# Three mask copies on ScalarE instead of GpSimd, and a shorter memset, in one inference step of a hybrid decoder

## The chip, the cores and the metric

The kernel runs on one core of one Trainium2 chip. The metric is device time in microseconds (us), the median of several runs; less is better. Engines in the profile: PE is TensorE (matmuls and transposes), PEld its weight loads, DVE is VectorE, ACT is ScalarE, POOL is GpSimd, SP is SyncE, which issues most of the DMAs. Each engine works through its own instruction stream in order; engines wait for each other by semaphores.

## The reference, cut to what matters

One decoder layer for a prompt of 1024 tokens and 8 decode samples. A projection `w_in` (1024 x 3480) feeds three groups of heads: an NSA group (compressed blocks, selected blocks, sliding window), an RWKV-7 group and a memory cross-attention; the groups are gated, concatenated and projected back.

```
q_raw, kv_raw, g_raw, z_nsa, u_rw, z_rw, q_mem, z_mem = split_in(rms_norm(x, ln_g) @ w_in)
ck, cv = compress(rows4[:, :2])          # blocks of 32 rows, stride 16, a small MLP
s_c = q @ ck * SCALE, masked by cend <= qpos      # uses cmask
s_s = q @ k_sel, s_w = q @ k_win (window 512)     # masked by bmask
o = g0 * softmax(s_c) @ cv + g1 * softmax(s_s) @ v_sel + g2 * softmax(s_w) @ v_win
y = x + concat(o * silu(z_nsa), o_rw * silu(z_rw), o_mem * silu(z_mem)) @ w_out
```

The change is in how the two masks of the prompt's attention are brought from DRAM into their final tiles. `bmask` (128 x 1152, bf16) is an additive mask: its first 128 columns hold the edge of the window, the last 128 the causal triangle, and the 896 between them are zero. `cmask` (128 x 248) holds the mask of the compressed scores as two matmul operands.

## The kernel before, in words

The kernel has three phases. Phase 1 projects the prompt in column blocks of `w_in` (the matmuls named `p_pr`, in split precision: `whi`, `wlo` by `hi`, `lo`), and weaves into these blocks, by written-out generators, the RWKV recurrence, the memory's keys and values, the turning of the attention's keys, and the compression of the prompt's K/V rows. Phase 2 is the prompt's attention, phase 3 the samples' and the output projection. TensorE's order is written out by hand: `InOrder` (line 77) chains every matmul and transpose behind the one before (line 86, `_do`), so that TensorE can take nothing out of turn.

The change is in `prompt_cmp` (line 1308), the generator of the compression, which runs near the end of phase 1. It does the following, in program order.

- Line 1311 takes the slot `c4` for the tile `c_am` (128 x 504, f32), and line 1312 loads the three masks' data into it with one DMA on SP's queue. `slot` (line 1271) gives out one buffer for each name `c0` to `c7`: a later tile of the same name must wait until all users of the earlier one are done.
- Lines 1313 to 1318 fill `bmask`, a one-column tile `one`, and `cmask`, all on GpSimd. The three copies (lines 1315, 1316, 1318) read `c_am`.
- Lines 1319 to 1327 load the compression's weights and the rows to compress (`px`).
- Lines 1332 to 1342 turn those rows: four groups of four transposes write `p_xt`, and ScalarE copies each group to a tile `pxt` (line 1340). The first of these, `pxt0`, takes the slot `c4` again, which `c_am` has held. So the first `pxt` copy can't start before the last reader of `c_am` is done.
- `p_xt` and the turned keys `p_k` share the PSUM pool `pw`, which has three buffers (line 499). The third `p_xt` takes the buffer that the first `pxt` copy frees.

Around it stand other generators: `turn_keys` (line 1282) turns keys (`p_k`), splits them on ScalarE (`kh`, line 1294) and VectorE (`kl`, line 1295); `cmp_consts` (line 1062) turns the position encoding (`p_pe`), copies it on VectorE (`peT`, line 1073) and multiplies it by the weights (`p_pc`); `do_z` (line 312) evicts the gate columns (`zt`, lines 317 and 318). GpSimd also issues the stores of the RWKV output (`y_d`, line 1040), ahead of the masks in its stream.

The masks' first use is in phase 2: `bmask` in line 1478 and `cmask` in line 1394.

Of the kernel before, what the change touches and what calls it, by code (L numbers as in the profile page):

```python
# [14 lines left out]
AF = mybir.ActivationFunctionType  # L15
# [98 lines left out]
class Step:  # L114
# [1193 lines left out]
    def prompt_cmp(self):  # L1308
        nc, I, O = self.nc, self.I, self.O
        V, A, G, PE = nc.vector, nc.scalar, nc.gpsimd, self.te  # L1310
        am = self.slot(4, [128, 504], F32, "c_am")
        nc.sync.dma_start(am[:], I["c_at"][:, 0:504])
        G.memset(self.bmask[:], 0.0)
        G.memset(self.one[:], 1.0)
        G.tensor_copy(self.bmask[:, 0:128], am[:, 128:256])
        G.tensor_copy(self.bmask[:, 1024:1152], am[:, 0:128])
        self.cmask = self.kt.tile([128, 248], F32R, name="cmask")
        G.tensor_copy(self.cmask[:], am[:, 256:504])
        self.load_w1([self.slot(e, [128, 8, 2, 64], F32, f"w1s{e}") for e in range(2)])
        xs = []  # L1320
        src = O["nsa_rows_prompt"]
        for e in range(2):
            x = self.slot(2 + e, [128, 2, 8, 64], F32, f"px{e}")
            for g in range(2):
                nc.sync.dma_start(x[:, g], bass.AP(tensor=src.tensor, offset=src.offset + (2 * e + g) * 64,
                                                  ap=[[8 * 512, 128], [512, 8], [1, 64]]))
            xs.append(x)
        yield 4.0
        consts = self.cmp_consts()
        self.spawned.append(consts)  # L1330
        xts = []
        for e in range(2):
            xt = self.slot(4 + e, [128, 4, 2, 128], F32, f"pxt{e}")
            for jj in range(0, 4, 2):
                ps = self.pw.tile([128, 2, 2, 128], F32, name="p_xt", tag="w")
                for j in range(2):
                    for g in range(2):
                        PE.transpose(ps[:, j, g, :], xs[e][:, g, 2 * (jj + j):2 * (jj + j) + 2, :].rearrange("p a b -> p (a b)"),
                                     self.ident[:])
                A.activation(xt[:, jj:jj + 2], ps[:], AF.Copy)  # L1340
                yield
            xts.append(xt)
        hid = self.wk.tile([128, 2, 64], F32, name="phid")
        while consts.gi_frame:
            yield 0.5
        yield from self.compress(lambda e, m: xts[e][:, m % 4, :, m // 4::2], 2, hid)
        self.spawned.append(self.mem_turn())
        ck, cv = self.cmp_out(hid[:].rearrange("p n c -> p (n c)"))
        yield 6.0
        self.k_stack(ck, 1, self.ck[:, :, 0, :], self.ck[:, :, 1, :])  # L1350

        nc.gpsimd.memset(self.cvk[:], 0.0)
        for g in range(2):
            r = slice(g * 64, g * 64 + 64)
            A.activation(self.cvk[r, g], cv[r], AF.Copy)
        yield 4.0
# [1228 lines left out]
```

## Time and profile before

| | |
|---|---|
| runs | 929.98, 935.8, 934.21 us; median 934.21 |
| the profiled execution | 932.48 us, its span 930.7 us, mean granted TensorE clock 0.994 |
| busy PE / PEld | 890.9 us (96%) / 756.6 us (81%) |
| busy DVE / ACT / POOL | 645.9 us (69%) / 439.6 us (47%) / 189.9 us (20%) |
| DMA | 107.01 MB, mean 115 GB/s |

The rows of the profile's views are read like this. A row of a timeline has start and busy time in us, the engine, the line of the kernel, the operation, output and inputs, shapes, and the number of instructions merged; in brackets stands the engine's idle time before it and what ended it. Line 86 is the helper through which all of TensorE's work goes, so tiles tell more there than lines. A row of waits has the waiting engine and tile, what it waited for, then the total in us, the number of times and the longest. Matmuls are pipelined, so a row's busy time is longer than the distance to the next row's start; distances between starts are the better measure.

### The profile page before, as it was taken

To read this page: it belongs to the slowest core of one execution; us is meant where nothing else is said; L and a number is where in the kernel's file an instruction comes from. 1 tells how busy PE (TensorE), PEld (TensorE's weight loads), DVE (VectorE), ACT (ScalarE), POOL (GpSimd) and SP (SyncE) were. 2 spreads that over 40 slices of the span, in tenths; PEclk is the share of its full clock that TensorE was granted. 3 is DMA by queue.
4 is the path that set the end of the run, shared out by engine and by line. 5 is a ranking of instruction groups with operands and counts; after the bars stand their busy time and mean duration, and the time that the engine had idled before them with its cause. 6 is when DMAs were issued, how large, how long until landed. Compare 5 with 4: busy or idle time off the path is not lost.

```text
span 930.7 us, 24648 instructions
## 1 busy us (share of the span) xinstructions
PE 890.9 (96%) x9839; PEld 756.6 (81%) x9839; DVE 645.9 (69%) x2002; ACT 439.6 (47%) x1003; POOL 189.9 (20%) x283
## 2 busy tenths in 40 slices
PE   8999999999999999988998999999999998999998
PEld 8998888977878788757986788888887877887976
DVE  7768679954777459945556876666778986548454
ACT  7654324232443233223536577667567776324211
POOL 2000000000000000001103544454445766112010
PEclk9999999999999999999999999999999999999999
DMA  8521314141321204524738413332130027986561
GB/s 281 133 74 35 105 36 121 51 115 48 89 82 53 76 14 133 134 84 121 183 102 231 137 59 120 106 117 66 33 87 13 29 81 209 307 259 213 177 236 48
DMA packets 128298, 107.01 MB, mean 115 GB/s; under 512 B 26385, under 2 KB 113112, under 8 KB 128056
## 3 DMA queue, kind: packets, MB, share of 16 engines
q1 hardware_dynamic: 123096, 93.43, 34.3%
q0 software_dynamic: 3296, 10.75, 3.3%
q8 instruction: 78, 1.28, 0.6%
q10 hardware_dynamic: 1792, 1.26, 0.4%
q14 instruction: 36, 0.29, 0.1%
HBM read 84.72 MB, written 22.78 MB: 116 GB/s over the span
## 4 chain that ended last, share of the span: by engine, by line
PE 67%; DVE 18%; ACT 5%; issue 4%; DMA 3%; POOL 2%; SPq 1%; DVEq 0%; ACTq 0%; POOLq 0%
PE p_pr L86 24%; PE p_out L86 8%; PE p_s L86 5%; PE p_o L86 5%; PE p_pT L86 4%; PE p_pr L306 2%; PE p_hid L86 2%; ACT p L1485 2%; DVE p L1478 2%; DMA wraw<-in_w_in_dram 2%; PE p_it L86 1%; DVE wlo L283 1%; PE p_tk L86 1%; PE p_iy L86 1%; DVE pt L1446 1%
## 5 line engine op out<-in xcount | busy, mean ns | idle before, releaser
L86 PE MATMUL p_pr<-h,whi 128*128 128x512 f32 (+2 forms) x1168 | 282.2, 335 | 2.0 <-DVE zt L318 2.0
L86 PEld LDWEIGHTS p_pr<-h,whi 128*128 128x128 f32 x1168 | 190.2, 190 | 22.1 <-issue 2.8
L86 PE MATMUL p_pr<-h,wlo 128*128 128x512 f32 (+2 forms) x584 | 188.9, 326 | 1.1 <-DVE wlo L283 1.1
L1516 POOL TENSOR_SCALAR p<-p,fac,gates 128x640 f32<-128x640 f32 (+7 forms) x128 | 104.2, 826 | 89.4 <-DVE fac L1512 56.0
L86 PEld LDWEIGHTS p_pr<-h,wlo 128*128 128x128 f32 x584 | 109.8, 189 | 11.3 <-DVE wlo L283 1.5
L1485 ACT ACTIVATE p<-p,nm 128x640 f32<-128x640 f32 (+7 forms) x128 | 93.1, 729 | 40.7 <-DVE nm L1478 37.4
L86 PE MATMUL p_pT<-ident,p 128*128 128x128 f32 x528 | 71.9, 279 | 8.8 <-DVE pt L1446 4.0
L1104 POOL MEMSET w2d<- 128x128 f32 x1 | 0.2, 205 | 376.8 <-PE p_iy L86 376.8
L86 PEld LDWEIGHTS p_pT<-ident,p 128*128 128x128 f32 x528 | 56.6, 140 | 21.6 <-issue 5.9
L86 PE MATMUL p_o<-pt,vs 128*64 128x128 f32 x1056 | 67.9, 276 | 0.4 <-DVE cat L1554 0.4
L86 PE MATMUL p_s<-kh,qs 128*128 128x512 f32 (+3 forms) x191 | 64.8, 352 | 1.8 <-DVE nm L1478 1.6
L1478 DVE CUSTOM_DVE_ANT_0 p<-p_s,bmask 128x512 f32<-128x512 f32 (+7 forms) x96 | 60.6, 661 | 7.6 <-PE p_s L86 6.1
L282 ACT ACTIVATE whi<-wraw 128x1024 fp32r<-128x1024 f32 x34 | 36.0, 1059 | 62.3 <-PE p_pr L86 48.8
L86 PEld LDWEIGHTS p_o<-pt,vs 128*64 128x64 f32 x1056 | 57.0, 137 | 7.7 <-issue 4.2
L283 DVE TENSOR_TENSOR wlo<-wraw,whi 128x1024 fp32r<-128x1024 f32 x33 | 40.3, 1221 | 33.0 <-ACT whi L282 32.9
L86 PE MATMUL p_s<-kl,qs 128*128 128x512 f32 (+3 forms) x192 | 60.4, 334 | 0.0
L1446 DVE COPY pt<-p_pT 128x512 f32<-128x512 f32 (+1 forms) x72 | 48.2, 673 | 11.7 <-PE p_pT L86 11.5
L86 PE MATMUL p_out<-woh,chi 128*128 128x512 f32 x128 | 51.7, 404 | 0.0
L86 PE MATMUL p_out<-woh,clo 128*128 128x512 f32 x128 | 50.2, 392 | 0.4 <-DVE clo L2421 0.4
L86 PE MATMUL p_out<-wol,chi 128*128 128x512 f32 x128 | 49.9, 390 | 0.0
L1444 ACT ACTIVATE pt<-p_pT 128x512 f32<-128x512 f32 (+1 forms) x72 | 41.1, 577 | 14.2 <-PE p_pT L86 13.6
L86 PEld LDWEIGHTS p_s<-kh,qs 128*128 128x128 f32 x191 | 36.1, 189 | 5.5 <-DVE nm L1478 3.0
(546 smaller groups left out, 1779.5 us busy)
## 6 DMA issues: line engine op xcount, KB each, us to landing
wraw<-in_w_in_dram SPq DMA_DIRECT2D x34, 512.0 KB
pg<-in_c_pool_dram SPq DMA_DIRECT2D x32, 256.0 KB
pg<-in_c_pool_dram SPq DMA_DIRECT2D x48, 128.0 KB
x<-in_x_prompt_dram SPq DMA_DIRECT2D x8, 512.0 KB
z_d<-zt SPq DMA_DIRECT2D x16, 256.0 KB
cat<-z_d SPq DMA_DIRECT2D x8, 512.0 KB
xres<-in_x_prompt_dram POOLq DMA_DIRECT2D x16, 256.0 KB, 3.6
out_dram<-xres POOLq DMA_DIRECT2D x16, 256.0 KB, 3.0
```

What stands on the lines that cost most here:

```text
L86: self.last = getattr(self.engine, op)(*a, **k)
L282: nc.scalar.activation(hi[:, :, :n], raw[:, :, :n], AF.Copy)
L283: (low or nc.vector).tensor_tensor(lo[:, :, :n], raw[:, :, :n], hi[:, :, :n].bitcast(F32), op=OP.subtract)
L306: self.last_mm = self.pe.matmul(ps[:m, :b - a], w[:, k, :m], h[k][:, a:b], start=(k == 0 and i == 0), stop=(k == 7 and i == 2))
L1104: nc.gpsimd.memset(w2d[:], 0.0)
L1444: nc.scalar.activation(pt[:, :n], ps[:, :n], AF.Copy)
L1446: nc.vector.tensor_copy(pt[:, :n], ps[:, :n])
L1478: return V.tensor_tensor_reduce(halves(x), halves(ps), m, -1.0, 3.0e38, op0=OP.add, op1=OP.min, accum_out=nm[:, h, b:b + 1])
L1485: e = A.activation(x, x, AF.Exp, scale=-1.0, bias=nm[:, h, b:b + 1], accum_out=sm[:, h, b:b + 1])
L1516: nc.gpsimd.tensor_scalar(x, x, f[:, h, b:b + 1], gate[:, hd + h, 1 + b:2 + b], op0=OP.mult, op1=OP.mult)
```

## The change

ScalarE (`A`) makes the three copies out of `c_am`, as activations with the function Copy, instead of GpSimd (`G`); GpSimd's memset of `bmask` covers only the 896 middle columns, which the copies don't write.

```
-        G.memset(self.bmask[:], 0.0)
+        G.memset(self.bmask[:, 128:1024], 0.0)
         G.memset(self.one[:], 1.0)
-        G.tensor_copy(self.bmask[:, 0:128], am[:, 128:256])
-        G.tensor_copy(self.bmask[:, 1024:1152], am[:, 0:128])
+        A.activation(self.bmask[:, 0:128], am[:, 128:256], AF.Copy)
+        A.activation(self.bmask[:, 1024:1152], am[:, 0:128], AF.Copy)
         self.cmask = self.kt.tile([128, 248], F32R, name="cmask")
-        G.tensor_copy(self.cmask[:], am[:, 256:504])
+        A.activation(self.cmask[:], am[:, 256:504], AF.Copy)
```

On ScalarE, near the end of phase 1, between the eviction of a gate block (`zt`) and the first copy of the turned rows (`pxt`), the stream changes so:

```order
 L317 ACTIVATE zt<-p_pr 128x256
 L317 ACTIVATE zt<-p_pr 128x264
+L1315 ACTIVATE bmask<-c_am 128x128
+L1316 ACTIVATE bmask<-c_am 128x128
+L1318 ACTIVATE cmask<-c_am 128x248
 L1340 ACTIVATE pxt_6349<-p_xt 128x512
 L1294 ACTIVATE kh_6225<-p_k_6375 64x2x256
```

Three instructions stand between the last eviction of `zt` and the first `pxt`; all other rows of ScalarE keep their order.

On GpSimd the masks stand behind two stores of the RWKV output:

```order
 L1813 MEMSET gr 128x6
 L1040 DMA y_d<-y_c 128x256 x2
-L1313 MEMSET bmask 128x1152
+L1313 MEMSET bmask 128x896
 L1314 MEMSET one 128x1
-L1318 CAST cmask<-c_am 128x248
-L1315 CAST bmask<-c_am 128x128
-L1316 CAST bmask<-c_am 128x128
 L1352 MEMSET cvk 128x128
 L1370 TENSOR_TENSOR qhl<-q_6602,qhl 128x4x64 x3
```

The memset is shorter and the three casts are gone. The streams of TensorE, VectorE and SP are the same row for row.

## The prediction

> **What bounds the kernel now.** I began with the page's busy times and its chain of waits by engine.
>
> ```profile
> PE 890.9 (96%) x9839; PEld 756.6 (81%) x9839; DVE 645.9 (69%) x2002; ACT 439.6 (47%) x1003; POOL 189.9 (20%) x283
> PE 67%; DVE 18%; ACT 5%; issue 4%; DMA 3%; POOL 2%; SPq 1%; DVEq 0%; ACTq 0%; POOLq 0%
> ```
>
> TensorE is busy for 890.9 of 930.7 us, so the kernel is bound by it, and only some 40 us of its idle time are left to win. A change on GpSimd and ScalarE pays only where TensorE waits for it. So the next view is TensorE's waits over the whole span, and then those of ScalarE around the change (405 to 520 us).
>
> ```profile
> PE p_pT L86 <- DVE pt L1446: 4.0, 6, 1.1
> PE p_xt L86 <- ACT pxt L1340: 3.0, 1, 3.0
> PE p_w L83 <- DMA ident<-in_c_mat_dram: 2.7, 1, 2.7
> ...
> ACT pxt L1340 <- POOL bmask L1316: 4.9, 1, 4.9
> ```
>
> The longest single wait of TensorE in the whole execution, 3.0 us, is for a `pxt` copy of ScalarE, and that copy has itself waited 4.9 us for the last mask copy on GpSimd. The chain of waits, taken from 424 to 437 us, has both in order (start, us, what):
>
> ```profile
> 427.35 0.43 DVE y_c L1038
> ...
> 428.87 1.08 POOL bmask L1313
> ...
> 430.54 0.24 POOL bmask L1316
> ...
> 430.80 0.60 ACT pxt L1340
> 431.40 0.48 ACT kh L1294
> ...
> 431.91 0.68 DVE kl L1295
> 432.59 0.11 DVE peT L1073
> ...
> 432.74 1.89 PE p_pc L86 x32
> ```
>
> VectorE's last step of the RWKV output (427.35) releases a store that GpSimd issues; only behind this do the memset and the copies run, and only then may `pxt0` overwrite the slot of `c_am`. The masks' data has nothing to do with this wait: the timelines of SP, POOL and ACT show where each stood.
>
> ```profile
> 368.41 0.50 SPq L1312 DMA_DIRECT2D c_am<-in_c_at_dram  x1
> ...
> 428.32 0.55 POOL L1040 DMA_DIRECT2D y_d<-y_c  x1 [1.09 <-DVE y_c L1038]
> 428.87 1.08 POOL L1313 MEMSET bmask<- 128x1152 bf16 x1
> ...
> 429.90 0.40 POOL L1318 CAST cmask<-c_am 128x248 fp32r<-128x248 f32 x1
> ...
> 425.49 0.39 ACT L317 ACTIVATE zt<-p_pr 128x264 f32<-128x264 f32 x1 [2.92 <-PE p_pr L86]
> 430.80 0.60 ACT L1340 ACTIVATE pxt<-p_xt 128x512 f32<-128x512 f32 x1 [4.93 <-POOL bmask L1316]
> ```
>
> ScalarE is idle from 425.88 (425.49 + 0.39) to 430.80, and the load of `c_am` was issued 57 us before that. The new copies fall into this hole.
>
> **The change part by part: ScalarE.** The trace has no copy of just these shapes. Near it stand, by ScalarE's groups with shapes apart (mean ns last before the idle time):
>
> ```profile
> L1369 ACT ACTIVATE qhl<-q 128x256 fp32r<-128x256 f32 x6 | 2.1, 406 | 0.0
> L1014 ACT ACTIVATE y_c<-p_yy 128x128 f32<-128x128 f32 x4 | 0.8, 282 | 7.3 <-PE p_yy L86 7.3
> ```
>
> I take 0.28 us for each 128x128 copy and 0.40 for 128x248. Back to back they overlap a little: the four `y_c` are 0.8 us of busy time together, against 4 x 0.28, some 0.1 us saved at each joint. So the three end about 425.88 + 0.28 + 0.28 + 0.40 - 0.2 = 426.65, with no more than 0.1 us of error either way if they run at these rows' rates. As an upper end I take 0.60 us for each (the row of the 128x512 `pxt`), which makes 427.7. The Trainium skill, page "ScalarE: Activation LUTs", section "What ACT_TABLE_LOAD costs", gives 186 ns + 0.833 ns per column with immediate scale; an estimate from that is 293, 293 and 393 ns, and the sum would be the same; the trace's 406 ns at 256 columns agrees.
>
> The first `pxt` now waits only for ScalarE's own copies and for a `p_xt` that TensorE had turned before `zt`'s last block was done. It starts at 426.65 instead of 430.80 and ends at 427.25: **4.15 us earlier**. `kh`, `kl` and `peT` follow it at the distances of before. `p_pc` started 432.74 - 430.80 = 1.94 us behind `pxt`, so VectorE allows it from 428.6 on (429.65 at the upper end).
>
> **TensorE.** These are its rows around the wait, and the granted clock there (the windows' columns are length, busy times of PE, PEld, DVE, ACT, POOL, then PEclk, DMA share, GB/s).
>
> ```profile
> 428.06 0.39 PE L86 MATMUL p_pr<-h,wlo 128*128 128x512 f32 x1
> 431.45 1.12 PE L86 MATMUL p_xt<-ident,px 128*128 128x128 f32 x4 [3.00 <-ACT pxt L1340]
> 432.74 1.89 PE L86 MATMUL p_pc<-w1s,peT 128*2 128x128 f32 x32 [0.17 <-DVE peT L1073]
> 434.56 0.76 PE L86 MATMUL p_pr<-h,whi 128*128 128x512 f32 x2
> 435.16 0.39 PE L86 MATMUL p_pr<-h,wlo 128*128 128x512 f32 x1
> ...
> 435.86 0.40 PE L86 MATMUL p_pr<-h,wlo 128*128 128x512 f32 x1
> 436.10 0.60 PE L86 MATMUL p_k<-ident,kd 128*128 128x128 f32 x4
> 436.53 0.60 PE L86 MATMUL p_xt<-ident,px 128*128 128x128 f32 x4
> 436.88 0.72 PE L86 MATMUL p_pr<-h,whi 128*128 128x512 f32 x2
> 437.44 0.39 PE L86 MATMUL p_pr<-h,wlo 128*128 128x512 f32 x1
> ...
> 428.00:431.45 3.45, 0.45 (x2) 0.01 (x1) 0.00 (x0) 0.65 (x2) 2.59 (x7) 0.97 0.96 257
> 431.45:432.70 1.25, 1.12 (x4) 0.71 (x4) 0.78 (x2) 0.98 (x3) 0.00 (x0) 0.50 0.53 193
> 432.70:434.60 1.90, 1.86 (x33) 1.03 (x33) 0.69 (x1) 1.11 (x2) 0.00 (x0) 0.50 0.00 0
> ```
>
> The pause costs more than its 3.0 us: the clock fell to 0.50 and stayed there for the 3.15 us behind it. The mean of 0.97 over the 3.45 us before means 0.2 us at half clock, so it fell near 431.2, some 2.8 us after the last matmul's end at 428.45. The same four transposes that need 0.35 us from start to start at full clock (436.53 to 436.88) needed 1.29. Worked out by starts:
>
> - The pause: 431.45 - 428.06 = 3.39 us, against 0.24 where a transpose follows a `p_pr` without a wait (435.86 to 436.10). Saved 3.15.
> - `p_xt`: 1.29 us to the start of `p_pc` against 0.35. Saved 0.94. This puts `p_pc` at 428.30 + 0.35 = 428.65, just behind the 428.6 at which VectorE allows it; with ScalarE's upper end 1.0 us of it is lost again.
> - `p_pc`: 432.74 to 434.56 is 1.82 us at half clock. At full clock it is between 0.91 (all of it array time) and 1.82 (all of it issue). The transposes, also 128 columns long, gained more than twofold, so I take the lower side, 0.95. Saved 0.87.
> - The first two `p_pr` behind it: 434.56 to 435.16 is 0.60, against 0.56 from 436.88 to 437.44, also behind transposes. Saved 0.04.
>
> The sum is 3.15 + 0.94 + 0.87 + 0.04 = **5.0 us**; the bounds of these terms together are 3.1 (late copies, `p_pc` bound by issue) and 5.1.
>
> The Trainium skill has a rule for the half clock, page "TensorE: Matmul & The Clock Gate", Part 1: the array falls to half rate after an idle window of about 3.4 us, which runs freely, and warms up in one busy window of the same length. The trace agrees on the half and nearly on the length (0.2 + 3.15 us), but here a pause of 2.8 us was enough. By the rule taken strictly, so short a pause need not always cost the half clock; in executions of before without it the change would save the 3.15 and the 0.17 wait for `peT` alone, 3.3 us.
>
> **What else moves.** The buffer that `p_xt` needs is free at 427.25, a microsecond before TensorE wants it. The second `p_k` (436.10 before, 431.1 now) needs the buffer of the first, which VectorE's second `kl` frees:
>
> ```profile
> 433.25 0.69 DVE L1295 TENSOR_TENSOR kl<-p_k,kh 64x512 fp32r<-64x512 f32 x1 [0.56 <-ACT kh L1294]
> ...
> PE p_mo L86 <- DVE wlo L1180: 0.4, 1, 0.4
> ```
>
> It ended at 433.94 and would end at 429.8, in time. GpSimd loses three casts and a fifth of a memset, and nobody else waited for these rows; no gain counted. The loads that SP issued before the pause don't move with TensorE. In the windows their traffic, 193 GB/s up to 432.70, is 0 behind it, so the last has landed by then; if the keys for the second `p_k` were among the last, TensorE would wait from 431.1 to 432.7, which bounds this at 1.6 us. Three loads of keys were queued ahead of the rest, so I take nothing. Later loads are issued when ScalarE or VectorE free a buffer, so they move along; one that stays put would show as a longer wait of `p_mo` for a `wlo`, whose row (0.4 us before) stands above. Cost taken as nothing; the bound is the whole 5.0 us if one transfer were fixed in time.
>
> **The rivals.**
>
> 1. *Given back later.* If a transfer or the store and reload of the gates (`z_d`) keeps its time, TensorE runs into it 5 us sooner and waits. For: the attention starts behind such a round trip, in the chain of waits and SP's timeline
>
> ```profile
> 497.10 4.63 DMA z_d<-zt
> 501.82 1.58 POOL p L1516 x2
> ```
>
> Against: the store is issued right after `zt` of the last block, which TensorE sets. A gain of 0 to 2.5 us stays: 931.7 to 934.2.
>
> 2. *Slower.* The same, with the pause moved whole to the start of the attention: a pause of 5 us there is longer than the 2.8 us after which the clock fell above, and the half clock would cost again what it cost here, 0.94 + 0.87 + 0.04 less the 0.17 wait, some 1.7 us beyond what was won. It decides from a pause of about 2.8 us on; 932.5 + 1.7 for the profile, 935.9 for the median. Against it stands that SP issues `z_d` only behind an eviction, which moves too.
>
> 3. *The change doesn't free ScalarE.* The copies might wait for the DMA of `c_am`, or for one counted with it. GpSimd's L1318, which reads it too, started at 429.90 right behind the memset, so it had landed by then. With that latest time `pxt` starts at 430.7 and nothing is won: 934.1. The 57 us since its issue speak against it.
>
> 4. *Function tables.* Copy stands behind the Tanh of `zt`. The page on ScalarE, section "Table sets: the hidden batching unit", says that a switch of table sets costs about 2.7 us, but that copy is in every set. The trace has one load in all:
>
> ```profile
> L210 ACT ACT_TABLE_LOAD x1 | 1.3, 1283 | 1.8 <-issue 1.8
> ```
>
> Many Copy behind Tanh run without one. With one load of 1.28 us ahead of the copies `pxt` would start at 427.93, `p_pc` at 429.87 instead of 428.65, and the gain would be 3.8 us: 930.4.
>
> **How the numbers follow.** The profiled execution of before took 932.48 us, 1.73 below the median of 934.21; its sum gives 932.48 - 5.0 = 927.5. The forecast against the median is 934.21 - 5.0 = **929.2 us**. Chances: the forecast with a gain of 3.1 to 5.1 us 0.80; rival 1 0.10; rival 2 0.04; rival 3 0.03; rival 4 0.02; a gain far larger than TensorE's waits here 0.01. The three runs of before lie 4.2 below to 1.6 above their median, and the time after will scatter likewise. The range goes down to 929.2 less 3.5 for scatter, 925.7, and up to 933.0, through the smaller gains of the forecast and half of rival 1. One per cent, about what a measurement of this kernel can tell from no change, is 9.3 us, almost twice the gain; so within 1% has 0.92, faster 0.05 (scatter on top of the gain), slower 0.03.
>
> **What would show it.** In the changed kernel's profile the wait of `p_xt` for `pxt` is gone or under 0.2 us; three ACTIVATE rows of about 0.28, 0.28 and 0.40 us start near 425.9; `p_xt`, `p_pc` and `p_pr` follow each other within 2 us at a granted clock near 1.00; and the start of the attention (501.82 before) lies 5 us earlier. Wrong would be: a new wait of ScalarE ahead of L1315, a `p_pc` that still takes 1.8 us at full clock, or a wait for DMA near 480 or 497 that eats the shift.

## The result, and the profile after

The median of the changed kernel is 927.42 us (13 runs, 925.54 to 930.71), that of before, run beside it, 932.59 us (13 runs, 928.98 to 936.55). The ratio is 0.9944, with a 95% interval of 0.9928 to 0.996: 3.7 to 6.7 us less, and 5.2 us in the middle. The forecast was 5.0 us less, which from the first three runs of before, median 934.21, made 929.2 us. With thirteen runs before lies 1.6 us lower, and the changed kernel came out 1.8 us under the forecast. The forecast's range reached up to 933.0 and so holds the median of before as well: the time alone can't tell the forecast from no gain, and the account below rests on the ratio and on the traces.

TensorE's waits over the whole span of the changed kernel, longest first:

```profile
PE p_pT L86 <- DVE pt L1446: 3.7, 5, 1.1
PE p_w L83 <- DMA ident<-in_c_mat_dram: 2.8, 1, 2.8
...
PE p_pc L86 <- DVE peT L1073: 0.3, 1, 0.3
```

The 3.0 us of `p_xt` for `pxt` are gone from the list; `p_pc` waits for `peT` 0.3 us instead of 0.2. ScalarE's timeline shows the three copies in the hole between `zt` and `pxt`:

```profile
423.37 0.39 ACT L317 ACTIVATE zt<-p_pr 128x264 f32<-128x264 f32 x1 [2.91 <-PE p_pr L86]
423.65 0.30 ACT L1315 ACTIVATE bmask<-c_am 128x128 bf16<-128x128 f32 x1
423.85 0.30 ACT L1316 ACTIVATE bmask<-c_am 128x128 bf16<-128x128 f32 x1
424.06 0.40 ACT L1318 ACTIVATE cmask<-c_am 128x248 fp32r<-128x248 f32 x1
424.48 0.60 ACT L1340 ACTIVATE pxt<-p_xt 128x512 f32<-128x512 f32 x1
424.98 0.58 ACT L1294 ACTIVATE kh<-p_k 64x512 fp32r<-64x512 f32 x1
425.45 0.58 ACT L1340 ACTIVATE pxt<-p_xt 128x512 f32<-128x512 f32 x1
```

They take 0.30, 0.30 and 0.40 us, start 0.2 us behind each other, and `pxt` begins 0.72 us after `zt`'s end instead of 4.92. On TensorE, in the same places as in the prediction:

```profile
425.88 0.39 PE L86 MATMUL p_pr<-h,wlo 128*128 128x512 f32 x1
426.11 0.60 PE L86 MATMUL p_xt<-ident,px 128*128 128x128 f32 x4
426.96 1.06 PE L86 MATMUL p_pc<-w1s,peT 128*2 128x128 f32 x32 [0.25 <-DVE peT L1073]
427.94 0.74 PE L86 MATMUL p_pr<-h,whi 128*128 128x512 f32 x2
428.52 0.39 PE L86 MATMUL p_pr<-h,wlo 128*128 128x512 f32 x1
```

The whole execution scatters by several us, so the experiments are read by a **stretch** that scatters less (2.64, 2.60 and 2.68 us in three traces of the changed kernel): from the start of the last `p_pr` before the third `p_xt` to the start of the `wlo` row of `p_pr` behind `p_pc`. In before it is 435.16 - 428.06 = 7.10 us, here 428.52 - 425.88 = 2.64: 4.46 us less.

The two profiled spans differ by more, 930.7 against 923.8. Part of that is older than the change: the stretch already starts 2.18 us earlier (425.88 against 428.06), though the program up to there is the same. The windows of the clock show one reason. First before, then after:

```profile
322.00:326.00 4.00, 4.00 (x37) 3.77 (x37) 0.25 (x1) 0.36 (x1) 0.00 (x0) 0.57 0.43 141
```

```profile
322.00:326.00 4.00, 4.00 (x50) 3.69 (x49) 1.48 (x4) 0.96 (x3) 0.00 (x0) 1.00 0.55 176
494.00:497.00 3.00, 3.00 (x8) 2.29 (x8) 1.74 (x6) 1.95 (x6) 1.39 (x2) 0.50 0.90 268
```

The column before the DMA share is the granted clock. Before had a spell at half clock near 323 us; after had none there, but one at 494, at the start of the attention (both have one more near 276). One pair of traces can't say whether the second belongs to the change; the repeat of the changed kernel below does.

### The profile page after: what moved, and what is told of

Same layout as the page of the kernel before. It is cut to its first block, busy times and chain, and to the rows that moved or that the text cites. A ratio compares the mean times of both kernels' runs of the same rounds, so it can differ in the third digit from the quotient of the medians.

```text
span 923.8 us, 24649 instructions
## 1 busy us (share of the span) xinstructions
PE 889.5 (96%) x9839; PEld 756.4 (82%) x9839; DVE 646.1 (70%) x2002; ACT 440.1 (48%) x1006; POOL 188.7 (20%) x280
## 3 DMA queue, kind: packets, MB, share of 16 engines
q10 hardware_dynamic: 1792, 1.26, 0.5%
## 4 chain that ended last, share of the span: by engine, by line
PE 69%; DVE 19%; ACT 5%; issue 3%; DMA 2%; POOL 1%; SPq 1%; DVEq 0%; ACTq 0%; POOLq 0%
PE p_pr L86 23%; PE p_out L86 9%; PE p_s L86 5%; PE p_o L86 4%; PE p_pT L86 4%; PE p_hid L86 4%; PE p_pr L306 2%; DVE p L1478 2%; ACT p L1485 2%; PE p_it L86 1%; PE p_tk L86 1%; PE p_iy L86 1%; DVE pt L1446 1%; DVE wlo L283 1%; PE p_w L86 1%
```

## The experiments

My theory: the gain is the end of one wait. ScalarE's `pxt` had to wait for GpSimd only because it reuses the slot of `c_am`, and GpSimd's casts came late because they stood behind stores that wait for VectorE. The rivals: GpSimd's work was the cost in itself; ScalarE's copies are what counts; the half clock behind the pause is something else than a result of the pause.

### The copies on ScalarE, the memset full again

```
-        G.memset(self.bmask[:, 128:1024], 0.0)
+        G.memset(self.bmask[:], 0.0)
```

> The copies on ScalarE, but the memset covers all of bmask again, so the two bmask copies must wait for it. Measured by the stretch from the last p_pr before the pause to the second p_pr (wlo) behind p_pc: 7.10 us in before, 2.64 us after the change. Theory (ScalarE is freed only because its copies no longer share columns with GpSimd's memset): ScalarE waits for the memset, about 4 us behind zt, pxt starts about 0.3 us sooner than in before, stretch 6.7 to 7.0 us, total within 0.5 us of before. Rival (the three casts were the cost, the memset is free): stretch about 2.6 us, total 5 us under before.

Measured: 932.85 us, ratio 0.9999 (0.9979 to 1.0019); stretch 6.94 us (429.56 to 436.50). ScalarE's timeline:

```profile
427.37 0.41 ACT L1318 ACTIVATE cmask<-c_am 128x248 fp32r<-128x248 f32 x1
431.57 0.31 ACT L1315 ACTIVATE bmask<-c_am 128x128 bf16<-128x128 f32 x1 [3.79 <-POOL bmask L1313]
431.78 0.29 ACT L1316 ACTIVATE bmask<-c_am 128x128 bf16<-128x128 f32 x1
432.11 0.60 ACT L1340 ACTIVATE pxt<-p_xt 128x512 f32<-128x512 f32 x1
```

`cmask` is copied at once, but the copies into `bmask` wait 3.79 us for the memset of the same columns, and `pxt` behind them. Without the smaller memset the stretch is 0.16 us shorter, and the time shows no gain.

### The smaller memset alone

```
-        G.memset(self.bmask[:], 0.0)
+        G.memset(self.bmask[:, 128:1024], 0.0)
```

> Only the memset is limited to the middle columns; the copies stay on GpSimd. Theory: GpSimd still starts behind its two stores, the casts end about 0.2 us sooner, stretch 6.8 to 7.0 us, total within 0.5 us of before. Rival (what GpSimd does in 430 us is the cost in itself): a gain in proportion to the work taken away, 0.2 of 2.1 us of it, which is the same 0.5 us at most; a rival in which the full memset holds up something else would show a gain of over 1 us.

Measured: 932.31 us, ratio 0.9997 (0.9977 to 1.0016). `pxt` waits for GpSimd 4.70 us instead of 4.93, the 0.2 us expected. The stretch, 7.42 us (426.45 to 433.87), is longer than expected, and TensorE shows why:

```profile
429.74 0.66 PE L86 MATMUL p_xt<-ident,px 128*128 128x128 f32 x4 [2.90 <-ACT pxt L1340]
431.04 1.89 PE L86 MATMUL p_pc<-w1s,peT 128*2 128x128 f32 x32 [0.63 <-DVE peT L1073]
432.85 1.22 PE L86 MATMUL p_pr<-h,whi 128*128 128x512 f32 x2
433.87 0.51 PE L86 MATMUL p_pr<-h,wlo 128*128 128x512 f32 x1
```

The half clock came later than in before: 3.8 us after TensorE's last matmul ended (426.85 to 430.69), against 2.8 there (428.45 to 431.24). So `p_xt` ran at full rate (0.66 us), but the `p_pr` behind `p_pc` did not (1.02 us from start to start instead of 0.60). The pause brings the spell, but not always at the same distance. And `p_pc` started 1.30 us behind a `p_xt` at full rate, as far as behind the slow one of before (1.29), for it waited 0.63 us for `peT`: the half clock under `p_xt` cost nothing in before, since VectorE held `p_pc` anyway. Neither half of the change alone gains anything that the times show.

### The masks left to GpSimd, `c_am` in another slot

```
-        am = self.slot(4, [128, 504], F32, "c_am")
+        am = self.slot(5, [128, 504], F32, "c_am")
```

This is before with one number changed: the third `pxt` reuses `c_am`'s slot, not the first.

> Before, with c_am in slot c5 instead of c4: all mask work stays on GpSimd, but the first pxt no longer overwrites c_am; the third pxt does, which has 3 us more time. Theory (the wait is by the shared slot alone): the first pxt starts right behind its transposes, stretch 2.2 to 2.7 us, total 4 to 6 us under before, like the change. Rival (ScalarE's speed or GpSimd's relief makes the gain): stretch 7.1 us, total as before. A third outcome: the third pxt waits for GpSimd and TensorE with it, stretch about 4 to 5 us.

Measured: 927.88 us, ratio 0.9944 (0.9922 to 0.9965), the same as the change; stretch 2.67 us (428.08 to 430.75). The timelines of ScalarE and, in the last row, of GpSimd:

```profile
424.14 0.60 ACT L1340 ACTIVATE pxt<-p_xt 128x512 f32<-128x512 f32 x1 [1.47 <-PE p_xt L86]
425.61 0.39 ACT L317 ACTIVATE zt<-p_pr 128x264 f32<-128x264 f32 x1 [0.87 <-PE p_pr L86]
...
430.92 0.60 ACT L1340 ACTIVATE pxt<-p_xt 128x512 f32<-128x512 f32 x1 [1.26 <-POOL bmask L1316]
...
428.99 1.08 POOL L1313 MEMSET bmask<- 128x1152 bf16 x1
```

GpSimd does all its work as late and as slowly as before. The first `pxt` no longer waits for it, the third does for 1.26 us, and TensorE doesn't notice. So neither ScalarE's copies nor the relief of GpSimd made the gain, only the wait through the slot.

### The pause filled

```
+            if e == 1:
+                keep = self.pM.tile([128, 512], F32, name="p_keep", tag="m")
+                for _ in range(26):
+                    PE._do("matmul", keep[:, :128], self.ident[:], self.ident[:], start=True, stop=True)
```

> Before, with 26 needless 128x128 matmuls on TensorE in the pause (they write a PSUM tile that nobody reads). The wait for ScalarE stays. Theory (the half clock behind the pause comes from TensorE's idleness and costs p_pc 0.85 us): clock near 1.00 behind the pause, p_xt 0.6 us long instead of 1.12, p_pc still starts 1.94 us behind pxt, then takes 0.95 to 1.0 us instead of 1.82; stretch about 6.2 us. Rival (p_pc is bound by issue, or the half clock falls there anyway): p_pc 1.8 us, stretch 7.1 us.

This one missed its aim: each of these f32 matmuls stands as two rows in the trace (52 rows for 26 instructions, 0.11 us each), so they needed 5.8 us, more than the pause, and the stretch became 8.12 us (one run, 932.78 us). The clock did stay up: `p_pc` to `p_pr` took 0.98 us. With 13 of them:

> Before, with 13 needless 128x128 matmuls in the pause, each of which takes two passes of 0.11 us, so 2.9 us in all and a little shorter than the pause. Theory (the half clock comes from TensorE's idleness): clock near 1.00, p_xt 0.60 us long, p_pc starts 1.94 us behind pxt as before and takes 0.98 us instead of 1.82, stretch 6.2 to 6.3 us instead of 7.10. Rival: p_pc 1.8 us, stretch 7.1 us.

One run, 929.73 us; stretch 6.35 us (425.98 to 432.33).

```profile
426.20 3.06 PE L86 MATMUL p_keep<-ident 128*128 128x128 f32 x26
429.49 0.66 PE L86 MATMUL p_xt<-ident,px 128*128 128x128 f32 x4 [0.22 <-ACT pxt L1344]
430.78 1.06 PE L86 MATMUL p_pc<-w1s,peT 128*2 128x128 f32 x32 [0.64 <-DVE peT L1073]
431.76 0.73 PE L86 MATMUL p_pr<-h,whi 128*128 128x512 f32 x2
```

And the window of the clock that the prediction showed for before in two pieces:

```profile
431.45:434.60 3.15, 3.15 (x33) 2.53 (x21) 1.75 (x6) 1.12 (x3) 0.00 (x0) 1.00 0.00 0
```

`p_xt` still starts only when `pxt` is done, and `p_pc`, 1.29 us later as in before, when `peT` is; but TensorE is not idle meanwhile, and the clock is 1.00 where it was 0.50. `p_pc` takes 0.98 us instead of 1.82, and the first two `p_pr` 0.57 instead of 0.60: 0.87 us is the half clock as such. The stretch shows 7.10 - 6.35 = 0.75 of it, because in this trace the pause, from start to start, is 0.12 us longer (3.51 against 3.39). Of the 4.46 us that the change saved, the other 3.6 us are the two waits, for `pxt` and for `peT`. The needless matmuls alone win the 0.75 in the stretch; one run can't show it in the time.

### The change, with `peT` on ScalarE

The change left a wait of `p_pc` for `peT`. This kernel takes that copy off VectorE:

```
-        V.tensor_copy(pt[:].rearrange("p e s j -> p (e s j)"), ps[:, :32])
+        with self.tc.high_priority(offset=FIRST): nc.scalar.activation(pt[:].rearrange("p e s j -> p (e s j)"), ps[:, :32], AF.Copy)
```

> The change, with the copy peT on ScalarE right behind the second pxt instead of on VectorE behind kl. Theory (in the changed kernel p_pc waits 0.3 us for peT only because VectorE's kl stands behind y_c, its own last RWKV step): the wait of p_pc is gone, p_pc starts 0.35 to 0.45 us behind p_xt instead of 0.85, stretch 2.2 us instead of 2.64; total 0 to 0.6 us under the changed kernel, which the times can hardly show. Rival (peT is late for another reason, or ScalarE delays kh and with it the second p_k): stretch 2.6 us or more, or a new wait of p_k.

Measured: 928.46 us, ratio 0.9945 (0.9927 to 0.9964); stretch 2.33 us (428.59 to 430.92).

```profile
428.83 0.60 PE L86 MATMUL p_xt<-ident,px 128*128 128x128 f32 x4
429.36 1.06 PE L86 MATMUL p_pc<-w1s,peT 128*2 128x128 f32 x32
```

The wait is gone, 0.31 us of the stretch with it, and the time doesn't show it. `p_pc` starts 0.53 us behind `p_xt`, not 0.35: that is what these four transposes need when such matmuls follow.

### The slot, with `peT` on ScalarE

> All mask work on GpSimd with the full memset, c_am in slot c5, and peT on ScalarE. Theory (slot and VectorE's queue together are the whole stall): stretch 2.2 us, total 5 to 5.6 us under before, no engine but GpSimd pays for the masks. Rival (the third pxt, which now waits for GpSimd, holds TensorE): a wait of p_k or p_xt of up to 1 us behind p_pc, total 4 to 4.5 us under before.

Measured: 926.36 us, ratio 0.9926 (0.9911 to 0.994); stretch 2.31 us (428.39 to 430.70); TensorE waits for none of `p_xt`, `p_pc` or `p_k`. That looked better than the stretch can explain, so it was timed again beside the changed kernel:

> The changed kernel, timed beside the next one. Theory: ratio to before 0.994 to 0.996, stretch 2.6 us.

> Slot c5 and peT on ScalarE once more, timed beside the changed kernel on the same chip. Theory (the two stretches differ by 0.3 us and nothing else does): ratio to before 0.0003 to 0.0005 under that of the changed kernel, within its interval, stretch 2.3 us. Rival (the slot version gains something outside the stretch, as its 0.9926 against 0.9944 and 0.9945 suggests): again 0.0015 or more under the changed kernel's ratio.

The changed kernel came to 926.2 us, ratio 0.9937 (0.9915 to 0.9958), stretch 2.68 us; the slot version to 927.06 us, ratio 0.9935 (0.9909 to 0.9961), stretch 2.33 us. The lead did not come again; the two are the same within what the times tell.

### The changed kernel once more

> The changed kernel once more, one look. Theory: stretch 2.6 us again; the half-clock spells elsewhere (near 276 and 495 us in the first trace, near 276 and 323 in that of before) belong to the execution and not to the kernel, so that the one near 495 need not come again and the one near 323 may; the start of the stretch lies anywhere from 425.9 to 429.6 us. Rival (the change moves the spell from 431 to 495): the one near 495 comes again.

One run, 927.1 us; stretch 2.60 us (427.19 to 429.79). The clock's windows, to be set beside those of the two first traces:

```profile
320.00:324.00 4.00, 4.00 (x44) 3.73 (x39) 0.73 (x2) 0.36 (x1) 0.00 (x0) 0.60 0.64 193
494.00:497.00 3.00, 2.63 (x11) 1.51 (x9) 2.69 (x6) 3.00 (x8) 0.87 (x1) 1.00 1.03 314
```

The spell near 323 is there and the one near 494 is not, in the same program. So the spells outside the pause come and go with the execution; the change did not move one from 431 to 494. The start of the stretch lies between 425.88 and 429.56 us in the twelve traces of all the kernels. It goes with the spells ahead of it and not with the kernel: the six traces that have both the one near 276 and the one near 323 start the stretch at 428.06 or later, the six that have at most one of these two at 427.32 or sooner.

## Why the prediction was right, point by point

- *What bounds it.* Right: one wait of TensorE, with its cause in the reuse of a slot. Another slot number alone gives the same gain.
- *ScalarE's copies.* Predicted 0.28, 0.28 and 0.40 us and `pxt` 0.77 us behind `zt`; measured 0.30, 0.30, 0.40 and 0.72. The Trainium skill, page "ScalarE: Activation LUTs", section "What ACT_TABLE_LOAD costs", comes as near: an estimate from its figures is 0.293 and 0.393 us.
- *The pause.* Predicted 3.15 us saved; 426.11 - 425.88 is 0.23 against 3.39, so 3.16.
- *`p_xt`.* This term was mis-sized: 0.94 us predicted, 1.29 - 0.85 = 0.44 measured. 0.18 us of the miss is the pitch, taken from transposes ahead of a `p_pr` (0.35), where ahead of `p_pc` they need 0.53. The other 0.32 us is the wait for `peT`. "`kh`, `kl` and `peT` follow it at the distances of before" was wrong: VectorE had become the later one. The cause was misread too: the term set the 1.29 us of before against transposes at full clock, but in before `p_pc` was waiting for `peT` (0.17 us), and the filled pause shows the same 1.29 us with the transposes at full clock. So the 0.44 us that was saved is VectorE's. For the same reason the prediction's 3.3 us for a before without the half clock was too low: the filled pause against the changed kernel gives 3.7 (6.35 - 2.64), or 3.6 without its longer pause.

```profile
425.24 0.42 DVE L1038 TENSOR_TENSOR y_c<-y_c,yb 128x256 f32<-128x256 f32 x1
426.12 0.68 DVE L1295 TENSOR_TENSOR kl<-p_k,kh 64x512 fp32r<-64x512 f32 x1 [0.46 <-ACT pxt L1340]
426.73 0.17 DVE L1073 COPY peT<-p_pe 128x32 f32<-128x32 f32 x1
```

  `kh` was done at 425.56, yet `kl` started at 426.12. It stands behind `y_c`, the RWKV output's last step, which ended at 425.66, and began 0.46 us after it. The trace names a `pxt` as the releaser, which ended just before by chance: with the other slot, and a `kh` done 1.45 us before, `kl` again starts 0.46 us behind `y_c`. The prediction had the row of `y_c`, ending at 427.78 in before, and should have set `kl` behind it.
- *`p_pc` and the clock.* Predicted 0.95 us at full clock, measured 0.98; the granted clock is 1.00 through the stretch, and the two filled pauses, with no half clock behind them, show that the idle TensorE was the cause. The Trainium skill, page "TensorE: Matmul & The Clock Gate", Part 1, puts the half clock behind an idle window of about 3.4 us, which runs freely. All three traces with the pause left empty had shorter waits (3.00, 2.80 and 2.90 us), and the half clock came in each: on the length, the measurement decides. The free running agrees with the traces: the start of the spell differed against the pause, and it lies in steps of 3.41 us from the other spells of its execution (last section). The prediction's "2.8 us after which the clock fell" was therefore the distance in one trace and no fixed delay.
- *What else moves.* Right: nothing was given back. The third `p_xt` and the second `p_k` found their buffers free, and no wait for a load appeared (one of 0.5 us for `pg` in the repeat comes as well in the two kernels that keep the pause, 0.5 and 0.4 us). The start of the attention's masked scores moved from 495.50 to 488.50 in the traces, 2.18 us of it from before the stretch. GpSimd's first row there, the 501.82 that the prediction named, moved to 495.62; without the 2.18 that is 4.0 us and not the 5 forecast (4.8 and 4.1 in the two further traces of the changed kernel). TensorE's waits for that line came to 2.0 to 2.7 us in total in before and the two kernels that keep the pause, and to 1.7 to 2.8 in the changed kernel's three traces.
- *The rivals.* None came: no wait of ScalarE ahead of L1315, one table load in the whole execution as before, and no pause at the attention's start beyond the 0.7 us at most that TensorE waits there in one piece.
- *The sum.* 5.0 us predicted; the stretch gives 4.46, the times 5.2 with an interval that holds both. That the times came nearer to 5.0 than the stretch is luck: the half microsecond of `p_xt` was not there.

## What to carry to other kernels

A long wait between two engines that share no data can be one through memory: the tile that waits overwrites another tile, and its last reader stands late in a queue for reasons of its own. Moving that reader to an idle engine, or giving the tile another buffer, ends the wait alike; the second was here one number, and left the busy engine's work alone. When a wait is taken away, look up on every engine behind it what its own queue holds at the new time: what was hidden behind the wait (here `y_c` ahead of `kl`) sets the next bound. And before a slow row is priced, look at what the row behind it waited for: the slow `p_xt` cost nothing, since `p_pc` could not have started sooner.

## What the runs showed of the hardware that I had not expected

A pause of 3 us on TensorE cost more than itself: the half clock behind it took another 0.87 us. Half-clock spells also come with no such pause, as at 494 to 497 us, where TensorE's waits shortly before were no longer than 0.7 us, and they differ between executions of one program.

The spells keep to a grid. Each is 3.41 us long, and in all ten traces that have more than one, their starts lie whole multiples of 3.41 us apart: in before 274.23, 322.01 and 431.24, which is 14 and 32 steps (157.01 / 46 = 3.413). In the step ahead of the spell at the pause TensorE was busy for 0.62, 0.74 and 0.66 us of 3.41 (before and the two kernels that keep the pause empty), less than in any other full step up to 920 us. The steps ahead of all other spells had 1.4 to 2.2 us. But not every such step brings one: 397.11 to 400.52 in before has 1.78 us and no spell behind it. What decides there stays open, and so does whether a pause of 3 us that fell half into one step and half into the next would bring a spell.

The times scatter with the granted clock, of which one spell takes 0.0018 off the mean (half of 3.41 in 930 us). Of the 28 runs of before beside the first three experiments, the two with a mean of 0.998 took 928.09 and 930.14 us, the four with 0.990 took 935.08 to 936.68.

An f32 matmul of 128x128 with the identity stood as two rows of 0.11 us in the trace where a transpose stood as one. And `kl`, which waits for ScalarE and for VectorE's own earlier work, started 0.46 us behind the instruction ahead of it even where ScalarE had long been done; what this gap depends on was not tried.
